# Emptying the bank of value products with one copy, two banks for it in one branch, and fillers moved ahead of a group's first product

## The chip, the core and the metric

The kernel runs on one core of a Trainium2 chip. A core has TensorE (matrix products, PE in the profile; its loading of stationary operands is listed apart as PEld), VectorE (DVE), ScalarE (ACT), GpSimd (POOL) and SyncE (SP), which issues the transfers. PE writes its results to PSUM, which has eight banks of 128 rows by 512 float32 values; everything else lies in SBUF, in tiles of 128 rows. The metric is the time of one execution on the device in microseconds.

## What is computed

One layer of a hybrid encoder on 1024 tokens of 1024 channels. A combined projection gives queries, keys and values for two groups of eight heads of 64 channels, and two gates. Branch A is a softmax over a band of 9 chunks of 64 with a learned bias; branch B is stick-breaking attention, causal and without a softmax. Both are projected, gated, merged and projected again; two layer norms and a SwiGLU block follow.

```
h = x @ w_in;  qa, ka, va, qb, kb, vb, ga, gb = split(h)
y_a = chunk_band_attention(qa, ka, va, rel_bias) @ w_proj_a
y_b = stick_breaking_attention(qb, kb, vb) @ w_proj_b
mix = (sigmoid(ga + b_a) * y_a + sigmoid(gb + b_b) * y_b) @ w_out
x = layer_norm(ALPHA * x + mix)
x = layer_norm(ALPHA * x + (silu(g) * u) @ w_ffn_out),  g, u = split(x @ w_ffn_in)

chunk_band_attention:     probs = softmax(q k / 8 + bias, within the band);  out = probs @ v
stick_breaking_attention: A[t, s] = beta_ts * prod_{s<j<t} (1 - beta_tj), beta = sigmoid(q k / 8);  out = A @ v
```

## The kernel before

Products are made in float32 split into a rounded part and a remainder (`split`, L102: a copy on ACT, then a subtraction on DVE, L103 and L104). The order of the tokens is reversed on the host, so that a causal sum runs forward.

The attention stage walks over 16 heads, eight of branch A and then eight of branch B. Two heads that follow each other, a pair, share one result tile `yt` of 128 rows (head `h` of the pair has rows `64 h` to `64 h + 63`) by 1024 queries. For each head the weights are made in eight blocks of 128 queries (`soft_block`, `stick_block`): scores on PE (L455, L456) into a bank of tag `sc`, then ACT and DVE, then POOL. In branch B the DVE part is a running product (L523, L527), whose second operand `ident_ps` lies in PSUM: it takes one bank of tag `tr` when the first block of branch B is made, which happens while the last head of branch A is still being finished, and keeps it.

The sums over the values are made in two groups of four query blocks, `g` 0 and 1, with eight and four steps, so twelve steps a head. A step (`value_steps`, L531) has two parts. `turn` transposes up to four blocks of weights on PE into a `tr` bank (L550) and splits them into a tile `pt` (tag of four tiles), which frees the bank. `mult`, which is called LAG = 2 steps later, multiplies `pt` with the values into the group's bank of tag `pv`. The stationary operand is 128 columns wide, 64 of the values' rounded part and 64 of their remainder, so the bank's rows 0 to 63 and 64 to 127 hold two parts of the same result, which have to be added. After a group's last step ACT copies rows 64 to 127 into `yt` (L569), and DVE adds rows 0 to 63 from PSUM to it (L570). Only then is the bank free for the next group's first product (L563).

PSUM is shared out as follows: two banks for `mm`, two for `sc`, three for `tr`, one for `pv`.

```
SLOTS = dict(bw=9, pt=4, yt=3, qs=2, kh=2, kl=2, v=2, gt=3, kp=4, op=8, xt=16)
BANKS = dict(mm=2, sc=2, tr=3, pv=1)
```

Between the parts of the steps stand fillers, matmuls of the remaining gates (L412) and of branch A's projection (L597), that need nothing of the present head. `fill_until` takes them from a generator, 18 per head of branch A and 42 per head of branch B (`FILL`), spread evenly over the twelve steps: half of a step's share behind its `turn`, half behind the `mult` that is called in that step. `LEAD` says how many blocks of weights are begun by each step, ahead of the step that uses them.

The written order is not quite the order on the engines. The framework plans the instructions with durations and buffers of its own, and where it expects a buffer to be in use it puts other instructions of the same engine first. Each engine then works through its queue in the planned order, with waits where an operand or a buffer is not ready.

Of the kernel before, what the change touches and what calls it, by code (L numbers as in the profile page):

```python
# [14 lines left out]
ALU = mybir.AluOpType  # L15
# [3 lines left out]
P = 128  # L19
# [3 lines left out]
DH = 64  # L23
# [8 lines left out]
LO, HI = slice(0, HW), slice(HW, 2 * HW)  # L32
# [14 lines left out]
def hybrid_trunk_kernel(ctx: ExitStack, tc, x, xt, w_in, b_gate, rel_bias, w_proj,  # L47
# [6 lines left out]
    nc = tc.nc  # L54
# [7 lines left out]
    def slot(tag, name, dtype=F32):  # L62
        return pool.tile([P, 1024], dtype, tag=tag, name=name, bufs=SLOTS[tag])
# [10 lines left out]
    def bank(tag, name):  # L74
        return ps.tile([P, HW], F32, tag=tag, name=name, bufs=BANKS[tag])
# [5 lines left out]
    tr = nc.tensor.transpose  # L81
# [20 lines left out]
    def split(dst_h, dst_l, src):  # L102
        nc.scalar.copy(dst_h, src)  # L103
        nc.vector.tensor_tensor(dst_l, src, dst_h.bitcast(F32), ALU.subtract)  # L104
# [324 lines left out]
    def load_qk(hd):  # L429

        i, h = hd["i"], hd["h"]
        n = 2 * i + h
        q, k = (d[i][h * P:(h + 1) * P] for d in (q_dr, k_dr))
        for key, part in (("qs", None), ("kh", 0), ("kl", DH)):
            t = hd[key] = slot(key, f"{key}{n}", F32R)
            if part is None:
                dma(t.bitcast(F32), q)
            else:
                for half in (slice(0, DH), slice(DH, P)):
                    dma(t[half].bitcast(F32), k[part:part + DH])  # L440
        if hd["br"] == 0:
            hd["bias"] = rel_bias_tile(hd["n"])

    def load_v(hd):

        n = 2 * hd["i"] + hd["h"]
        t = slot("v", f"v{n}", F32R)
        dma(t.bitcast(F32), v_dr[n])
        hd["v"] = t.rearrange("p (t c) -> p t c", t=8)
# [81 lines left out]
    def value_steps(hd, g, wt):  # L531

        br, h = hd["br"], hd["h"]
        reach = (4, 8)[br]
        q0 = 4 * g
        nm = f"{'ab'[br]}{hd['n']}_{g}"
        pv = []

        kbs = [4, 5, 6, 7, 3, 2, 1, 0] if g == 0 else [7, 6, 5, 4]
        steps = []  # L540
        for i, kb in enumerate(kbs):
            lo_q = max(q0, kb - reach)
            hi_q = min(q0 + 3, kb)
            n = (hi_q - lo_q + 1) * P
            pts = []

            def turn(kb=kb, lo_q=lo_q, hi_q=hi_q, n=n, pts=pts):
                tp = bank("tr", f"tp_{nm}_{kb}")
                for qb in range(lo_q, hi_q + 1):
                    tr(tp[:, (qb - lo_q) * P:(qb - lo_q + 1) * P],  # L550
                       wt[qb - q0][:, (kb - qb) * P:(kb - qb + 1) * P], ident)
                pt = slot("pt", f"pt_{nm}_{kb}", F32R)
                split(pt[:, 0:n], pt[:, HW:HW + n], tp[:, 0:n])
                pts.append(pt)

            def mult(i=i, kb=kb, lo_q=lo_q, n=n, pts=pts):
                v = hd["v"]
                if i == 0:
                    pv.append(bank("pv", f"pv_{nm}"))
                last = i == len(kbs) - 1  # L560
                cs = slice((lo_q - q0) * P, (lo_q - q0) * P + n)
                pt = pts[0]
                mm(pv[0][:, cs], v[:, kb, :], pt[:, 0:n], start=(i == 0), stop=False)  # L563
                mm(pv[0][:, cs], v[:, kb, :], pt[:, HW:HW + n], start=False, stop=last)
                if last:
                    yt = hd["yt"]()
                    r = slice(h * DH, (h + 1) * DH)
                    gs = slice(g * HW, (g + 1) * HW)
                    nc.scalar.copy(yt[r, gs], pv[0][DH:P])  # L569
                    nc.vector.tensor_tensor(yt[r, gs], pv[0][0:DH], yt[r, gs], ALU.add)  # L570
                    if h == 1 and g == 1 and hd["i"] < 7:
                        dma(y_dr[hd["i"]], yt)

            steps.append((turn, mult))
        return steps


# [56 lines left out]
    def fill_until(t):  # L634
        while state["t"] < t and not state["done"]:
            try:
                state["t"] += next(fill)
            except StopIteration:
                state["done"] = True
# [29 lines left out]
    pend = []  # L669
    steps_of = {}  # L670
    nhead = 12
    goal = 0.0
    load_qk(heads[0])
    load_v(heads[0])
    for si, (hd, g, st, box) in enumerate(vsteps):
        hidx, pos = si // nhead, si % nhead
        if hidx < 15 and pos == 1:
            load_qk(heads[hidx + 1])
        if hidx < 15 and pos == 4:
            load_v(heads[hidx + 1])  # L680
        while wi < min(hidx * 8 + LEAD[pos], len(wunits)):
            wunits[wi]()
            wi += 1
        if st == 0:
            steps_of[(hidx, g)] = value_steps(hd, g, box)
        turn, mult = steps_of[(hidx, g)][st]
        turn()
        last = goal
        goal += FILL[hd["br"]] / nhead
        fill_until(0.5 * (last + goal))  # L690
        pend.append(mult)
        if len(pend) > LAG:
            pend.pop(0)()
        fill_until(goal)
    for m_ in pend:
        m_()
    yh[7], yl[7] = slot("xt", "yh7", F32R), slot("xt", "yl7", F32R)
    split(yh[7], yl[7], last_yt[0])
# [226 lines left out]
```

## Time and profile before

| what | value |
|---|---|
| median of 3 runs | 1505.68 us (1505.52 to 1507.96) |
| the profiled execution | 1505.5 us, span 1503.5 us |
| projections, up to branch A's first value products | 0 to 359 us |
| branch A's value steps | 359 to 491 us |
| branch B's value steps | 493 to 684 us |
| everything after | 684 to 1503 us |
| groups drained | 16 in branch A, 16 in branch B |

In the profile a row of a wait reads "engine, tile, line <- engine, tile, line that released it: us in total, times, longest". A row in the order of time reads "start, duration, engine, line, operation, output <- inputs, shape, count", with the idle time of the engine before it and what ended it in brackets. Rows that follow each other on one engine and are of one kind are merged, so that the duration of two is given as one. PE rows overlap each other, since matmuls are pipelined; PEld rows are the loading of the stationary operand and run beside the matmul before.

### The profile page before, as it was taken

How to read it: one execution, taken by the hardware profiler on the slowest of the kernel's cores; microseconds unless marked ns; L12 is line 12 of the kernel's file. 1: busy time of each engine (PE TensorE's matmuls, PEld its weight loads, DVE VectorE, ACT ScalarE, POOL GpSimd, SP SyncE). 2: the span in 40 equal slices, each digit the busy share in tenths (PEclk: the TensorE clock that was granted, in tenths of full speed). 3: DMA queues.
4: the chain of work that ended last, by engine and by line, in shares of the span. 5: the costliest groups of instructions: out<-in, count | busy, mean ns of one | idle time of the engine just before them, and what ended most of it. 6: DMA issues, size and time to landing. Idle time of an engine off the chain costs nothing.

```text
span 1503.5 us, 18765 instructions
## 1 busy us (share of the span) xinstructions
PE 1455.7 (97%) x6824; PEld 1194.9 (79%) x6824; DVE 956.5 (64%) x1566; ACT 654.2 (44%) x1118; POOL 234.0 (16%) x290
## 2 busy tenths in 40 slices
PE   8999999999999999899999899999999999999997
PEld 6788888887887777777787688888888888888886
DVE  8865556436778887887749975555555447254437
ACT  6444444336778778775303643333333334021201
POOL 0000000004445568650014000000000000000016
PEclk9999999999999999999999999999999999999999
DMA  6555555247755556548402132222222248033202
GB/s 210 166 171 168 168 168 168 98 151 208 209 162 141 168 155 215 177 168 281 167 14 85 60 136 84 85 84 84 85 84 84 84 149 297 31 127 98 70 7 106
DMA packets 59324, 202.07 MB, mean 134 GB/s; under 512 B 7632, under 2 KB 7632, under 8 KB 59232
## 3 DMA queue, kind: packets, MB, share of 16 engines
q1 hardware_dynamic: 59232, 200.89, 41.2%
q8 instruction: 53, 0.87, 0.2%
q14 instruction: 39, 0.32, 0.1%
HBM read 141.06 MB, written 59.80 MB: 134 GB/s over the span
## 4 chain that ended last, share of the span: by engine, by line
PE 78%; DVE 11%; ACT 3%; DMA 3%; issue 3%; POOL 2%; SPq 0%; POOLq 0%; DVEq 0%; ACTq 0%
PE sxf L165 15%; PE sxp L165 11%; PE szf L165 8%; PE szp L165 6%; PE fps L113 5%; PE fps L110 5%; PE fps L111 5%; PE syf L165 4%; PE syp L165 3%; PE gps L412 2%; DVE kp_b L527 2%; PE ops L113 2%; PE ops L111 2%; PE ops L110 2%; PE yAps L597 1%
## 5 line engine op out<-in xcount | busy, mean ns | idle before, releaser
L739 POOL TENSOR_TENSOR mv<-mv,neghalf 128x1 f32<-128x1 f32 x16 | 23.4, 1460 | 760.6 <-DVE mv L738 760.6
L110 PE MATMUL fps<-wh_fo,wh_h 128*128 128x512 f32 x352 | 136.9, 389 | 0.0
L111 PE MATMUL fps<-wl_fo,wh_h 128*128 128x512 f32 x352 | 136.9, 389 | 0.0
L113 PE MATMUL fps<-wh_fo,wl_h 128*128 128x512 f32 x352 | 136.9, 389 | 0.0
L887 DVE TENSOR_TENSOR x<-fps,x 128x512 f32<-128x512 f32 x80 | 55.0, 689 | 96.2 <-PE fps L113 96.2
L529 POOL TENSOR_TENSOR w_b<-w_b,kp_b 128x511 f32<-128x511 f32 (+3 forms) x96 | 97.7, 1024 | 51.4 <-DVE kp_b L527 40.5
L527 DVE TENSOR_TENSOR_SCAN kp_b<-kp_b,ident_ps 128x384 f32<-128x384 f32 (+6 forms) x88 | 78.3, 890 | 4.1
L111 PEld LDWEIGHTS fps<-wl_fo,wh_h 128*128 128x128 f32 x352 | 66.1, 188 | 13.8
L113 PEld LDWEIGHTS fps<-wh_fo,wl_h 128*128 128x128 f32 x352 | 66.1, 188 | 13.6
L110 PEld LDWEIGHTS fps<-wh_fo,wh_h 128*128 128x128 f32 x352 | 66.1, 188 | 13.6
L395 ACT CAST wh_h<-wr_h 128x1024 fp32r<-128x1024 f32 x22 | 23.1, 1052 | 116.8 <-PE fps L111 50.7
L519 ACT ACTIVATE kp_b<-sc_b 128x512 f32<-128x512 f32 (+3 forms) x96 | 48.4, 504 | 31.4 <-PE sc_b L456 27.4
L178 DVE TENSOR_TENSOR c<-sxp,c 128x512 f32<-128x512 f32 x16 | 11.1, 691 | 74.8 <-issue 41.6
L104 DVE TENSOR_TENSOR pt_b<-tp_b,pt_b 128x512 fp32r<-128x512 f32 (+1 forms) x96 | 51.0, 542 | 11.0 <-ACT pt_b L103 10.5
L165 PE MATMUL szf<-x1S63h,wcf 128*128 128x512 f32 x176 | 57.8, 389 | 0.0
L550 PE MATMUL tp_b<-ident,w_b 128*128 128x128 f32 x288 | 49.4, 277 | 5.2 <-DVE pt_b L104 2.9
L473 POOL MEMSET bias<- 64x64 f32 x8 | 1.2, 145 | 334.1 <-ACT bias L472 334.1
L103 ACT CAST pt_b<-tp_b 128x512 fp32r<-128x512 f32 (+1 forms) x96 | 47.1, 497 | 13.9 <-PE tp_b L550 13.4
L494 POOL TENSOR_SCALAR w_a<-w_a,st_a 128x640 f32<-128x640 f32 (+2 forms) x64 | 42.6, 671 | 67.5 <-DVE st_a L493 49.9
L178 DVE TENSOR_TENSOR gt<-sxf,gt 128x512 f32<-128x512 f32 x22 | 15.1, 688 | 59.2 <-PE sxf L165 59.2
L113 PE MATMUL ops<-wh_o,ml 128*128 128x512 f32 x128 | 50.2, 392 | 0.2 <-DVE ml L104 0.2
L104 DVE TENSOR_TENSOR pt_a<-tp_a,pt_a 128x512 fp32r<-128x512 f32 (+1 forms) x96 | 45.4, 484 | 7.6 <-ACT pt_a L103 7.3
(1658 smaller groups left out, 4346.7 us busy)
## 6 DMA issues: line engine op xcount, KB each, us to landing
wLf<-in_w_ffn_in_dram SPq DMA_DIRECT2D x22, 512.0 KB, 3.5
wRf<-in_w_ffn_in_dram SPq DMA_DIRECT2D x22, 512.0 KB, 3.5
h_dr<-h SPq DMA_DIRECT2D x22, 512.0 KB, 2.6
wr_h<-h_dr SPq DMA_DIRECT2D x22, 512.0 KB, 4.4
wr_fo<-in_w_ffn_out_dram SPq DMA_DIRECT2D x22, 512.0 KB, 4.4
wLp<-in_w_in_dram SPq DMA_DIRECT2D x17, 512.0 KB, 5.2
wRp<-in_w_in_dram SPq DMA_DIRECT2D x17, 512.0 KB, 4.2
v_dr<-v SPq DMA_DIRECT2D x16, 512.0 KB, 4.2
```

What stands on the lines that cost most here:

```text
L103: nc.scalar.copy(dst_h, src)
L104: nc.vector.tensor_tensor(dst_l, src, dst_h.bitcast(F32), ALU.subtract)
L110: mm(acc, lh, rh, start=(i == 0), stop=False)
L111: mm(acc, lh, rl, start=False, stop=False)
L113: mm(acc, ll, rh, start=False, stop=(i == n))
L165: mm(acc, lw[:, ks], rx, start=(first and kt == i == 0), stop=(kt == 3 and i == 2), skip_group_check=not first)
L494: nc.gpsimd.tensor_scalar(s[:, 0:w], s[:, 0:w], st[:, 3:4], 0.0, ALU.mult, ALU.add)
L519: nc.scalar.activation(kp[:, c0:e], sc[:, 0:n], AF.Sigmoid, scale=-1.0)
L527: nc.vector.tensor_tensor_scan(kp[:, s0:e], kp[:, s0:e], ident_ps()[:, 0:e - s0], kp[:, s0 - 1:s0], ALU.mult, ALU.bypass)
L529: nc.gpsimd.tensor_tensor(be[:, m0:e], be[:, m0:e], kp[:, m0 - 1:e - 1], ALU.mult)
L550: tr(tp[:, (qb - lo_q) * P:(qb - lo_q + 1) * P], wt[qb - q0][:, (kb - qb) * P:(kb - qb + 1) * P], ident)
L887: nc.vector.tensor_tensor(acc_t[tt][:, cs], acc, acc_t[tt][:, cs], ALU.add)
```

## The change

Three things are changed in the attention stage.

First, the drain of a `pv` bank. ACT copies all 128 rows of the bank to SBUF, and DVE adds the two halves from there, so the bank has one reader. For the first head of a pair the copy goes to the pair's own `yt`, whose rows 64 to 127 are written later by the second head; for the second head it goes to a scratch tile `yv` from the same tag of three tiles, of which the first 512 columns are used. The addition's two inputs are then both in SBUF, rows 0 to 63 and rows 64 to 127.

Second, in branch A the second group of each head takes its bank from tag `tr`, so that the groups take it from `pv` and `tr` by turns. The number of banks of each tag stays. Branch B takes all from `pv`.

Third, before a group's first value product the rest of the step's fillers is taken ahead of the product; before, it stood behind it.

```diff
@@ value_steps
             def mult(i=i, kb=kb, lo_q=lo_q, n=n, pts=pts):
                 v = hd["v"]
                 if i == 0:
-                    pv.append(bank("pv", f"pv_{nm}"))
+
+                    pv.append(bank("tr" if br == 0 and g == 1 else "pv", f"pv_{nm}"))
                 last = i == len(kbs) - 1
...
                     gs = slice(g * HW, (g + 1) * HW)
-                    nc.scalar.copy(yt[r, gs], pv[0][DH:P])
-                    nc.vector.tensor_tensor(yt[r, gs], pv[0][0:DH], yt[r, gs], ALU.add)
+                    both, cs = (yt, gs) if h == 0 else (slot("yt", f"yv_{nm}"), LO)
+                    nc.scalar.copy(both[:, cs], pv[0])
+                    nc.vector.tensor_tensor(yt[r, gs], both[0:DH, cs], both[DH:P, cs], ALU.add)
                     if h == 1 and g == 1 and hd["i"] < 7:
                         dma(y_dr[hd["i"]], yt)
 
-            steps.append((turn, mult))
+            steps.append((turn, mult, i == 0))
         return steps
@@ the loop over the steps
-        turn, mult = steps_of[(hidx, g)][st]
+        turn, mult, begins = steps_of[(hidx, g)][st]
         turn()
         last = goal
         goal += FILL[hd["br"]] / nhead
         fill_until(0.5 * (last + goal))
-        pend.append(mult)
+        pend.append((mult, begins))
         if len(pend) > LAG:
-            pend.pop(0)()
+            m_, begins = pend.pop(0)
+            if begins:
+
+                fill_until(goal)
+            m_()
         fill_until(goal)
-    for m_ in pend:
+    for m_, _ in pend:
         m_()
```

## The prediction

> **What bounds the kernel now.** I read the page first, then busy time by stage, then who waited for whom in the two attention stages, then single drains in the order of time.
>
> ```profile
> PE 1455.7 (97%) x6824; PEld 1194.9 (79%) x6824; DVE 956.5 (64%) x1566; ACT 654.2 (44%) x1118; POOL 234.0 (16%) x290
> PE   8999999999999999899999899999999999999997
> ```
>
> TensorE (PE) is busy in nearly every slice, so the kernel can only get shorter where PE's remaining holes are. Busy time of each engine in the two stages that the change touches (branch A from 359 to 491 us, branch B from 505 to 684 us) says where these are:
>
> ```profile
> 359.00:491.00 132.00, 126.05 (x760) 106.21 (x759) 107.20 (x354) 104.93 (x262) 56.71 (x92) 1.00 0.61 171
> 505.00:684.00 179.00, 166.17 (x895) 133.81 (x896) 147.21 (x248) 136.24 (x292) 109.83 (x139) 1.00 0.56 177
> ```
>
> The columns are length, then PE, PEld, DVE, ACT, POOL. PE has 5.95 us without a matmul in A and 12.83 us in B; the granted clock is 1.00, so it plays no part. DVE is 82% busy in B, so it is the next engine in line. Who waited (total us, times, longest), branch A's rows first:
>
> ```profile
> PEld tp_a L550 <- DVE pt_a L104: 3.5, 7, 1.1
> PE tp_a L550 <- DVE pt_a L104: 2.3, 6, 0.9
> PE pv_a L563 <- DVE yt L570: 0.4, 1, 0.4
> ```
> ```profile
> PEld pv_b L563 <- DVE yt L570: 13.0, 13, 2.1
> PE pv_b L563 <- DVE yt L570: 8.1, 10, 1.6
> PEld tp_b L550 <- DVE pt_b L104: 7.8, 13, 1.1
> PE tp_b L550 <- DVE pt_b L104: 2.9, 6, 0.7
> ```
>
> In B the greatest wait of PE, 8.1 of its 12.83 us, is the first value product of a group (L563) waiting for the one `pv` bank, which the addition on DVE (L570) releases. One such drain, in order of time:
>
> ```profile
> 505.90 0.28 PE L564 MATMUL pv_b<-pt_b,v 128*128 128x128 f32 x1
> 506.62 0.58 ACT L569 COPY yt<-pv_b 64x512 f32<-64x512 f32 x1
> 507.33 0.39 PE L412 MATMUL gps<-xh,wh_g 128*128 128x512 f32 x1
> 507.56 0.40 PE L412 MATMUL gps<-xl,wh_g 128*128 128x512 f32 x1
> 507.69 0.53 DVE L104 TENSOR_TENSOR pt_b<-tp_b,pt_b 128x384 fp32r<-128x384 f32 x1
> 508.14 0.67 DVE L570 TENSOR_TENSOR yt<-pv_b,yt 64x512 f32<-64x512 f32 x1
> 508.74 0.40 DVE L523 TENSOR_TENSOR_SCAN kp_b<-kp_b,ident_ps 128x128 f32<-128x128 f32 x1
> 508.86 0.19 PEld L563 LDWEIGHTS pv_b<-pt_b,v 128*128 128x128 f32 x1 [1.33 <-DVE yt L570]
> 508.86 0.50 PE L563 MATMUL pv_b<-pt_b,v 128*128 128x512 f32 x1 [0.90 <-DVE yt L570]
> 509.17 0.61 DVE L527 TENSOR_TENSOR_SCAN kp_b<-kp_b,ident_ps 128x192 f32<-128x192 f32 x1
> 509.70 0.40 DVE L104 TENSOR_TENSOR pt_b<-tp_b,pt_b 128x256 fp32r<-128x256 f32 x1
> 511.05 0.59 PEld L550 LDWEIGHTS tp_b<-ident,w_b 128*128 128x128 f32 x4
> ```
>
> The last product of the old group ends at 506.18. ACT has its half out by 507.20. The addition stands behind other DVE work until 508.14 and ends at 508.81; the next group's product starts at 508.86. PE's loss lies between the two marks, 0.90 and 1.33. Over branch B it therefore lies between 8.1 and 13.0 us; I take the middle, 10.5.
>
> **The change part by part.** *The drain.* Each of the 32 groups keeps one ACT copy and one DVE addition; the copy takes 128 rows in place of 64, the addition reads SBUF alone in place of PSUM and SBUF. Groups by shape (busy us, mean ns), with the nearest rows of the new shapes:
>
> ```profile
> L569 ACT COPY yt<-pv_b 64x512 f32<-64x512 f32 x16 | 9.3, 582 | 0.6
> L191 ACT COPY c<-sxp 128x512 f32<-128x512 f32 x16 | 9.4, 589 | 29.3 <-PE sxp L165 29.3
> L570 DVE TENSOR_TENSOR yt<-pv_b,yt 64x512 f32<-64x512 f32 x16 | 10.8, 678 | 1.5 <-ACT yt L569 1.3
> L142 DVE TENSOR_TENSOR tbp<-wLp,tbp 128x512 f32<-128x512 f32 x16 | 10.9, 683 | 0.0
> ```
>
> So a copy grows by 7 ns and an addition by 5 ns: 0.2 us on each engine over 32 groups, beside PE work, taken as nothing. The bank is now free at the end of the copy, 507.20 in the drain shown. PE would have begun the product's weights at 507.53 (508.86 less the idle 1.33), so this wait goes entirely. It goes too in the longest stall of the stage:
>
> ```profile
> 633.07 0.58 ACT L569 COPY yt<-pv_b 64x512 f32<-64x512 f32 x1
> 636.02 0.19 PEld L563 LDWEIGHTS pv_b<-pt_b,v 128*128 128x128 f32 x1 [2.06 <-DVE yt L570]
> 636.99 0.40 DVE L104 TENSOR_TENSOR pt_b<-tp_b,pt_b 128x256 fp32r<-128x256 f32 x1
> 638.22 0.59 PEld L550 LDWEIGHTS tp_b<-ident,w_b 128*128 128x128 f32 x4
> ```
>
> There the copy ends at 633.65 and the product was wanted at 633.96. The margins are 0.33 and 0.31 us.
>
> What is late next: PE arrives earlier at the four transposes of the next head's first step, and these need a bank from which DVE's subtraction (L104) two steps back must have read. In the first drain that subtraction ends at 510.10 and the transposes start at 511.05, so PE can gain 0.95 us there at most; in the second it ends at 637.39 and they start at 638.22, 0.83 us. DVE's rows from 507.69 on follow one another without a hole, so it cannot bring that subtraction forward. The stalls themselves lie between 0.90 and 1.33 in the one, 1.63 (the longest of the PE row) and 2.06 in the other, with middles of 1.12 and 1.85. Of 2.97 us then 1.78 are kept, 60%. Of 10.5 us that is 6.3 us: my value for B. The bounds are 0 (DVE gives nothing back) and 13.0 (all of it).
>
> *The scratch tile.* For the odd head of a pair the copy goes to a tile of its own from the three `yt` slots. The pair's result holds one, two copies the others, and the earliest of them is long read when the next pair begins; no load waits for it, and the store of a pair (L572) is as far behind the addition as before. Nothing on SP's or POOL's queue moves.
>
> *The fillers.* Up to half a step's filler matmuls move from behind the first value product to ahead of it: 1.75 of them in B (42/12/2), 0.75 in A. Their number is the same, so PE's work is the same. In the drain shown two fillers follow each other at 507.33 and 507.56, 0.23 us apart, so 1.75 of them give the copy 0.40 us more, beside the margins of 0.33 and 0.31. I count no cost: what the product holds meanwhile, its `pt` tile, is one of four. Were the fourth `pt` tile missing, the step after would wait by those 0.40 us in each of 16 groups, 6.4 us over B.
>
> *Two tags in A.* A's own waits for the bank are 0.4 us by the PE row, and they go. That they are so few comes from the order on PE, which is not the written one:
>
> ```profile
> 404.26 0.20 PEld L550 LDWEIGHTS tp_a<-ident,w_a 128*128 128x128 f32 x2
> 405.67 0.58 ACT L569 COPY yt<-pv_a 64x512 f32<-64x512 f32 x1
> 406.37 0.67 DVE L570 TENSOR_TENSOR yt<-pv_a,yt 64x512 f32<-64x512 f32 x1
> 406.68 0.60 PE L550 MATMUL tp_a<-ident,w_a 128*128 128x128 f32 x4
> 406.97 0.41 DVE L104 TENSOR_TENSOR pt_a<-tp_a,pt_a 128x256 fp32r<-128x256 f32 x1
> 407.12 0.19 PEld L563 LDWEIGHTS pv_a<-pt_a,v 128*128 128x128 f32 x1
> ```
>
> The planner has put the next group's first product (407.12) behind transposes of two later steps (406.68), so the drain is covered by other work. The price of the second tag is a `tr` bank: while a second group of a head accumulates there, transposes have two banks in place of three, for some four of a head's twelve steps, 32 steps in all. Branch B shows what two banks cost, since `ident_ps` holds the third there: 2.9 us of PE waits over 96 steps, so 1.0 us over 32 steps; this I take, as the nearest row. Ends: at the worst the two transposes of 404.26 wait until the copy has emptied the bank at 406.25, 2.0 us in each of 7 heads, 14 us; at the best A's whole tp wait of 2.3 us goes with the new order.
>
> In the last head of A `ident_ps` has a `tr` bank already, and one is left for transposes:
>
> ```profile
> 485.90 0.33 PE L550 MATMUL tp_a<-ident,w_a 128*128 128x128 f32 x1 [0.40 <-DVE pt_a L104]
> 488.12 0.94 PE L550 MATMUL tp_b<-ident,w_b 128*128 128x128 f32 x4
> 488.99 0.27 DVE L104 TENSOR_TENSOR pt_a<-tp_a,pt_a 128x128 fp32r<-128x128 f32 x1
> ```
>
> The transposes at 488.12 would have to wait for the subtraction that ends at 489.26: 1.1 us, once. It may be nothing, if the planner finds other work, or three turns of it, 3.4.
>
> *The addition on DVE.* In the list from A the addition ends at 407.04 and the next DVE instruction starts at 406.97: they overlap by 0.07 us. I take no loss here. The Trainium skill, page "VectorE: DVE Perf Modes", section "Two Vector instructions with no wait between them", says that an instruction whose input or output starts in another 32-partition group than the last is held until all earlier ones have finished, and the new addition reads rows 0 to 63 and 64 to 127 of SBUF. No row of before has such a pair of inputs. By that rule each of B's 16 additions would lose that overlap, some 1.1 us on DVE, and were all of it on the path the sum would be 1.1 us higher.
>
> **The sum.** Against the profiled execution of 1505.5 us (span 1503.5; the median of the runs is 1505.68, 0.2 us off): minus 6.3 (B), minus 0.4 (A's wait), plus 1.0 (two banks in A), plus 1.1 (last head of A) is minus 4.6, so 1500.9 us.
>
> **The rivals.** *DVE takes the time back.* For it speaks DVE's 82% in B and the unbroken row of DVE work after each stall; against it the 0.95 and 0.83 us of room. B then gives 0, and the sum is 1505.5 - 0.4 + 2.1 = 1507.2.
>
> *A drain that is still late.* The margins are 0.3 us, and a copy that stands one ACT cast (0.58) later brings the wait back in part. If half of B's gain goes so, the time is 1505.5 - 3.2 - 0.4 + 2.1 = 1504.0; the change would then not do what it says, though the fillers' 0.4 us speak against it.
>
> *Branch A loses more by the third transpose bank than B gains* (slower). Place: the transposes just after a second group's last product. Price: up to 2.0 us a head. It ends above no change when 7 heads cost more than 6.3 + 0.4 - 1.1 = 5.6 us, 0.8 a head, and measurably above from 1.23. At 1.5 us a head the time is 1505.5 - 6.7 + 1.1 + 10.5 = 1510.4. Against it: PE had fillers, scores and other transposes to run in that very stretch. The Trainium skill, page "Perfetto Trace Analysis", section "Optimization Strategy", says that the same gap repeating can mean too little PSUM for the next tile; it fits the stalls in B as well as this rival, where the gap would appear at the transposes.
>
> **How the numbers follow.** Forecast 0.55, own range 1495 to 1503; DVE takes it back 0.15; late drain 0.12; slower by the bank 0.18. The range for all is 1495 (B near 10.5, A unchanged) to 1510 (the bank rival at about 1.5 a head). A measurement tells 0.2%, 3 us, from no change. Faster has nearly all of the forecast and a little of the late drain: 0.56. Same has the rest of these and most of the first rival: 0.24. Slower: 0.20.
>
> **What would show it.** Right: the row of L563 waiting for DVE L570 is gone, no row of it waiting for ACT above 2 us, and B's length falls by 5 to 7 us, with more waiting of transposes for DVE's `pt_b`. Wrong: A longer than 134 us with transposes waiting for ACT L569 or `pt_a`; a wait of L563 for ACT; or DVE rows in B with holes behind the addition. As the order on PE is planned anew, a loss outside both stages would also make the prediction wrong.

## The result and the profile after

The changed kernel takes 1510.65 us (median of 7 runs, 1508.55 to 1514.99), the kernel before 1505.19 us on the same chip (7 runs, 1503.9 to 1507.96). The ratio is 1.0038 with a 95% interval of 1.0024 to 1.0052: the change costs 0.4%. The prediction was 1500.9 us and faster. The profiled execution of the changed kernel has a span of 1508.1 us, against 1503.5. One execution each of `e2_tags`, `e6_psum_const` and `e9_scan_first` below was disturbed (1811.53, 2068.99 and 8307.96 us): the ratios leave it out, and the profile of `e6_psum_const`, which fell on it, is not shown.

In the totals of the page (busy time, share of the span, instructions), PE is nearly as it was, and DVE has grown by 11.5 us with the same number of instructions:

```profile
PE 1457.2 (97%) x6824; PEld 1196.8 (79%) x6824; DVE 968.0 (64%) x1566; ACT 649.8 (43%) x1118; POOL 237.3 (16%) x290
```

Busy time in the two stages (length, PE, PEld, DVE, ACT, POOL, clock):

```profile
359.00:491.00 132.00, 125.28 (x749) 104.58 (x747) 109.17 (x353) 101.34 (x258) 56.55 (x90) 1.00 0.60 170
505.00:684.00 179.00, 162.09 (x875) 132.08 (x874) 152.32 (x244) 130.40 (x286) 112.69 (x140) 0.99 0.54 170
```

In the same 179 us of branch B, PE does 162.09 us of work where it did 166.17, and DVE is busy for 152.32 where it was for 147.21. DVE has rather fewer instructions there (244 for 248) and needs 5 us more for them. The clock column of branch B has gone from 1.00 to 0.99. That is one stretch of 3.4 us at half the clock:

```profile
642.00:645.40 3.40, 3.29 (x11) 2.93 (x12) 2.58 (x5) 1.64 (x2) 1.99 (x3) 0.50 0.00 0
```

By estimate it costs at most 1.7 us (half of 3.4), and it begins at the end of the transposes' longest wait for DVE, 2.52 us. In the kernel before neither branch has such a stretch; what sets one off was not tried. Who waited in branch B (us in total, times, longest):

```profile
PE tp_b L550 <- DVE pt_b L104: 14.7, 13, 2.5
PEld tp_b L550 <- POOL w_b L529: 12.6, 8, 2.9
PEld tp_b L550 <- DVE pt_b L104: 8.2, 17, 1.1
PEld pv_b L564 <- ACT yv_b L571: 0.3, 1, 0.3
PEld pv_b L564 <- ACT yt L571: 0.2, 1, 0.2
```

The row that the change aimed at is gone: no value product waits for DVE any more, and for the new copy on ACT (L571) only 0.5 us. In its place the transposes wait for DVE's subtraction, 14.7 us where it was 2.9, and their loading for GpSimd's weights, 12.6 us where it was 2.2. GpSimd's own instruction is fed by DVE's scans (L527), but its total wait for them is no longer than before (29.3 us between 505 and 684 us, before 33.9), so the scans alone do not explain why GpSimd is late. The drain that the prediction showed reads, in order of time:

```profile
507.05 0.27 PE L565 MATMUL pv_b<-pt_b,v 128*128 128x128 f32 x1
507.61 0.65 ACT L571 COPY yt<-pv_b 128x512 f32<-128x512 f32 x1
508.83 0.53 DVE L104 TENSOR_TENSOR pt_b<-tp_b,pt_b 128x384 fp32r<-128x384 f32 x1
508.95 0.19 PEld L564 LDWEIGHTS pv_b<-pt_b,v 128*128 128x128 f32 x1
509.06 1.16 POOL L529 TENSOR_TENSOR w_b<-w_b,kp_b 128x448 f32<-128x448 f32 x1 [0.38 <-DVE kp_b L527]
509.40 1.37 DVE L572 TENSOR_TENSOR yt<-yt 64x512 f32<-64x512 f32 x1
510.69 0.41 DVE L523 TENSOR_TENSOR_SCAN kp_b<-kp_b,ident_ps 128x128 f32<-128x128 f32 x1
511.13 1.60 DVE L527 TENSOR_TENSOR_SCAN kp_b<-kp_b,ident_ps 128x192 f32<-128x192 f32 x2
512.65 0.40 DVE L104 TENSOR_TENSOR pt_b<-tp_b,pt_b 128x256 fp32r<-128x256 f32 x1
513.19 0.63 PE L550 MATMUL tp_b<-ident,w_b 128*128 128x128 f32 x4 [1.77 <-DVE pt_b L104]
```

The early part is as predicted. The bank is free at 508.26, the next product's weights load at 508.95 with no wait in front. But the addition takes 1.37 us where it took 0.67, and it began (509.40) while a multiplication on GpSimd (509.06 to 510.22) was under way. PE's gain of about a microsecond is given back at the transposes of 513.19, which stand idle for 1.77 us behind the subtraction of 512.65. A second thing differs: the subtraction (`pt_b`, 128x256) now stands behind the next block's second scan; in the kernel before it stood between the two scans (in the prediction's list of this drain the scan of 509.17 stands before it, and another follows at 510.02). So there were two suspects.

All additions of the changed kernel (duration in ns: least, median, greatest; then first and last start):

```profile
L572 DVE TENSOR_TENSOR yt<-yt x16: 686/774/2520, 367.6 to 674.1; 64x512 f32<-64x512 f32 x16
L572 DVE TENSOR_TENSOR yt<-yv_a x8: 689/690/1099, 382.5 to 493.2; 64x512 f32<-64x512 f32 x8
L572 DVE TENSOR_TENSOR yt<-yv_b x8: 689/1118/1384, 534.2 to 690.7; 64x512 f32<-64x512 f32 x8
```

The least is 686 ns, as predicted (683). Half of them are longer. Their busy time, by groups of line and shape, is 17.9 + 6.2 + 8.8 = 32.9 us; the kernel before had 10.9 + 10.8 = 21.7:

```profile
L572 DVE TENSOR_TENSOR yt<-yt 64x512 f32<-64x512 f32 x16 | 17.9, 1119 | 0.8 <-ACT yt L571 0.3
L572 DVE TENSOR_TENSOR yt<-yv_b 64x512 f32<-64x512 f32 x8 | 8.8, 1105 | 1.2 <-ACT yv_b L571 1.0
L572 DVE TENSOR_TENSOR yt<-yv_a 64x512 f32<-64x512 f32 x8 | 6.2, 778 | 0.5 <-ACT yv_a L571 0.2
```

Of 32 additions 16 take more than 0.75 us. Each of the 16 begins while a GpSimd instruction that reads SBUF is under way. Set against the time that this instruction still has to run, the durations lie on one line (us; the first two are the list above and the longest of all):

| addition at | GpSimd still runs for | addition takes | difference |
|---|---|---|---|
| 509.40 | 0.82 (L529) | 1.37 | 0.55 |
| 567.49 | 1.98 (L626) | 2.52 | 0.54 |
| 438.53 | 1.53 (L396) | 2.08 | 0.55 |
| 542.71 | 0.55 (L529) | 1.10 | 0.55 |
| 621.92 | 0.28 (L396) | 0.83 | 0.55 |
| 388.59 | 0.44 (L494) | 0.98 | 0.54 |

So the addition behaves as if it stood still until GpSimd is done and then took another 0.55 us. Two more additions began less than 0.12 us before the end of a GpSimd instruction and took 0.69 and 0.72. In the kernel before, where one input came from PSUM, 17 additions began inside such an instruction with more than 0.28 us to run (508.14 above: GpSimd runs from 507.91 to 509.04), and none was longer than 0.69 us. By the Trainium skill, page "SBUF — State Buffer", section "Who interferes with whom", a DVE instruction with two SBUF inputs contends with a GpSimd instruction that reads SBUF. The section "SBUF: two separate sides" of that page of the Trainium skill says that whichever of the two starts first gets the shared pair of ports for the whole instruction and that the other blocks. The table agrees with it on the blocking of DVE. The trace agrees on the other direction too, as one stretch shows:

```profile
516.08 2.40 POOL L396 TENSOR_TENSOR wl_y<-wr_y,wh_y 128x1024 fp32r<-128x1024 f32 x1 [0.22 <-PE gps L412]
517.79 1.24 DVE L572 TENSOR_TENSOR yt<-yt 64x512 f32<-64x512 f32 x1
518.43 1.48 POOL L529 TENSOR_TENSOR w_b<-w_b,kp_b 128x383 f32<-128x383 f32 x1
```

The addition stands behind the first GpSimd instruction, and the second one, which begins inside the addition, takes 1.48 us; in the kernel before the same multiplication took 1.01 us beside the old addition. Five multiplications of branch B begin inside an addition and take 0.43 to 0.46 us more than their shape usually takes, 2.2 us in sum. So GpSimd is late in part by the same lock.

### The profile page after: what moved, and what is told of

The parts are those of the page before. It is cut to its first block, busy times and chain, and to the rows that moved or that the text cites. A ratio compares the mean times of both kernels' runs of the same rounds, so it can differ in the third digit from the quotient of the medians.

```text
span 1508.1 us, 18751 instructions
## 1 busy us (share of the span) xinstructions
PE 1457.2 (97%) x6824; PEld 1196.8 (79%) x6824; DVE 968.0 (64%) x1566; ACT 649.8 (43%) x1118; POOL 237.3 (16%) x290
## 4 chain that ended last, share of the span: by engine, by line
PE 81%; DVE 11%; ACT 3%; issue 2%; POOL 1%; DMA 1%; POOLq 0%; SPq 0%; DVEq 0%; ACTq 0%
PE sxf L165 15%; PE sxp L165 11%; PE szf L165 8%; PE szp L165 6%; PE fps L110 5%; PE fps L111 5%; PE fps L113 5%; PE syf L165 4%; PE syp L165 3%; DVE kp_b L527 2%; PE gps L412 2%; PE yAps L599 2%; PE ops L113 2%; PE ops L111 2%; PE ops L110 2%
## 5 line engine op out<-in xcount | busy, mean ns | idle before, releaser
L529 POOL TENSOR_TENSOR w_b<-w_b,kp_b 128x511 f32<-128x511 f32 (+3 forms) x96 | 100.3, 1049 | 54.4 <-DVE kp_b L527 35.0
L527 DVE TENSOR_TENSOR_SCAN kp_b<-kp_b,ident_ps 128x384 f32<-128x384 f32 (+6 forms) x88 | 78.4, 891 | 4.6
L550 PE MATMUL tp_b<-ident,w_b 128*128 128x128 f32 x288 | 49.9, 280 | 17.6 <-DVE pt_b L104 14.7
L550 PEld LDWEIGHTS tp_b<-ident,w_b 128*128 128x128 f32 x288 | 34.1, 141 | 32.3 <-POOL w_b L529 12.6
L494 POOL TENSOR_SCALAR w_a<-w_a,st_a 128x640 f32<-128x640 f32 (+2 forms) x64 | 43.2, 679 | 67.8 <-DVE st_a L493 48.1
L110 PE MATMUL ops<-wh_o,mh 128*128 128x512 f32 x128 | 50.2, 392 | 0.0
```

The costliest lines, as they stand in the source:

```text
L110: mm(acc, lh, rh, start=(i == 0), stop=False)
L494: nc.gpsimd.tensor_scalar(s[:, 0:w], s[:, 0:w], st[:, 3:4], 0.0, ALU.mult, ALU.add)
L527: nc.vector.tensor_tensor_scan(kp[:, s0:e], kp[:, s0:e], ident_ps()[:, 0:e - s0], kp[:, s0 - 1:s0], ALU.mult, ALU.bypass)
L529: nc.gpsimd.tensor_tensor(be[:, m0:e], be[:, m0:e], kp[:, m0 - 1:e - 1], ALU.mult)
L550: tr(tp[:, (qb - lo_q) * P:(qb - lo_q + 1) * P], wt[qb - q0][:, (kb - qb) * P:(kb - qb + 1) * P], ident)
```

## The experiments

Three theories were to be told apart for the loss. *The lock*: the addition's second SBUF input makes it wait for GpSimd. *The banks* (K in some expectations): the `tr` bank that branch A gives away costs the time, the prediction's own rival. *The order* (O): the planner's new place for the subtraction costs it. A fourth, smaller one is that the two inputs start in different rows. Runs made together share a chip and a set of runs of the kernel before: 1504.5 us for the first four, 1504.33 for `e6`, `e8`, `e9` and `e11`, 1504.2 for the others. A line `...` in an edit marks what is left out.

**Part 1 alone: the drain.**

```diff
-                    nc.scalar.copy(yt[r, gs], pv[0][DH:P])
-                    nc.vector.tensor_tensor(yt[r, gs], pv[0][0:DH], yt[r, gs], ALU.add)
+                    both, cs = (yt, gs) if h == 0 else (slot("yt", f"yv_{nm}"), LO)
+                    nc.scalar.copy(both[:, cs], pv[0])
+                    nc.vector.tensor_tensor(yt[r, gs], both[0:DH, cs], both[DH:P, cs], ALU.add)
```

> The first part alone: one copy of 128 rows on ACT, then the addition from SBUF on DVE; tags and fillers as before. Theory L (the addition with both inputs in SBUF stands still while a GpSimd tensor_tensor on SBUF runs, so that DVE falls behind and the transposes wait for the subtraction two steps back): slower than before by 2 to 6 us, additions in branch B of about 1.4 us at the median, 10 us or more of PE waits of tp_b for DVE pt_b. Theory K (the loss is the bank that the second tag takes): faster by 3 us or more. Theory O (the loss is the order that the moved fillers bring): faster by 3 us or more.

Measured: 1512.25 us, ratio 1.0048 (1.0034 to 1.0062). The additions and the wait behind them:

```profile
L571 DVE TENSOR_TENSOR yt<-yt x16: 686/914/2523, 366.8 to 675.9; 64x512 f32<-64x512 f32 x16
L571 DVE TENSOR_TENSOR yt<-yv_b x8: 689/1118/1380, 535.9 to 692.5; 64x512 f32<-64x512 f32 x8
PE tp_b L550 <- DVE pt_b L104: 14.9, 13, 2.5
```

The whole loss comes with the drain alone, somewhat more than the 2 to 6 us that the theory of the lock expected, and with it the long additions. Branch B has two stretches at half the clock here (514.1 and 643.8, 3.4 us each), worth at most 3.4 us of the loss. The banks fall as its cause.

**Part 2 alone: two tags in branch A.**

```diff
-                    pv.append(bank("pv", f"pv_{nm}"))
+                    pv.append(bank("tr" if br == 0 and g == 1 else "pv", f"pv_{nm}"))
```

> The second part alone: the second group of a head in branch A takes its bank from tag tr. Theories L and O: within 2 us of before. Theory K: slower by 3 to 6 us, and the loss lies in branch A.

Measured: 1504.54 us, ratio 0.9998 (0.9989 to 1.0007): nothing. In branch A transposes wait 1.4 us for `pt_a` where they waited 2.3; in branch B the waits stay (8.1 us for the bank, 2.9 for `pt_b`).

**Part 3 alone: the fillers.** The old drain and tag, with the fillers taken ahead of a group's first value product.

```diff
...
+            if begins:
+                fill_until(goal)
+            m_()
```

> The third part alone: fillers ahead of a group's first value product, drain and tags as before. Theory L: faster by 2 to 6 us, since 1.75 fillers of 0.23 us go into 16 stalls of branch B (up to 6.4 us). Theory O: slower by 2 us or more. Theory K: as L.

Measured: 1503.41 us, ratio 0.9989 (0.998 to 0.9997), a gain of 1.1 us. The wait that it shortens was 8.1 us, 10 times:

```profile
PE pv_b L564 <- DVE yt L571: 6.9, 10, 1.4
```

So 1.2 us, or 0.08 for each of 16 groups. That is below what each theory had expected here (a gain or a loss of 2 us or more). The prediction had counted 0.40 us of margin a group; why so much less of it arrives was not tried.

**Parts 2 and 3, the old drain.**

> The second and the third part with the old drain. Theory L: faster by 2 to 6 us, the sum of the two alone; additions of 0.68 us throughout. Theories O and K: slower by 2 us or more, so that the drain isn't what makes the change slower.

Measured: 1503.91 us, ratio 0.9991 (0.9982 to 1.0). The changed kernel differs from this one by the drain alone and is 0.47% slower in relation to the kernel before, so the drain costs about 7 us on top of the other parts too. The gain of 0.09% is again below the 2 us expected.

**The drain with its second input from PSUM.** In branch B the addition takes its second input from `ident_ps`, a PSUM bank that is there anyway. All else is the changed kernel; the sum over the remainder rows is left out.

```diff
-                    nc.vector.tensor_tensor(yt[r, gs], both[0:DH, cs], both[DH:P, cs], ALU.add)
+                    nc.vector.tensor_tensor(yt[r, gs], both[0:DH, cs], aside[0][0:DH] if br else both[DH:P, cs], ALU.add)
```

> The changed kernel, but in branch B the addition takes ident_ps in PSUM as its second input in place of rows 64 to 127 of the copy (that half of the value product is left out). The bank is still free after the copy; the addition has one input in SBUF; and the planner puts the subtraction of step 10 ahead of the next block's last scan again, as before the change. Theories L (the addition stands still while GpSimd reads SBUF) and O (the subtraction of step 10 stands behind one scan more): faster than before by 2 to 8 us, additions of 0.68 us throughout. Theory Q (it is the early release itself that brings PE into other waits): still slower by 2 us or more.

Measured: 1501.2 us, ratio 0.9977 (0.9968 to 0.9986). With the lock gone the change is a gain of 0.2%. The planner also put the subtraction back to its old place here, so this run alone does not part lock from order.

**The same, with the order of the changed kernel.** As above, and the subtraction of step 10 is tied behind the second scan of the next head's fourth block.

```diff
...
+                scan = scans.get((hd["n"] + 1, 3)) if br == 1 and g == 1 and kb == 5 else None
+                with tc.issue_after(scan.ins) if scan else ExitStack():
+                    split(pt[:, 0:n], pt[:, HW:HW + n], tp[:, 0:n])
```

> As the kernel with ident_ps as second input (half of the value product of branch B left out), but the subtraction of step 10 is tied behind the last scan of the next head's block 3, so that DVE has the order of the changed kernel without its long additions. Theory L: within 2 us of before or faster. Theory O: slower than before by 3 us or more, near the changed kernel.

Measured: 1501.04 us, ratio 0.9978 (0.9969 to 0.9988). The additions, and the drain of before in order of time:

```profile
L575 DVE TENSOR_TENSOR yt<-yt,ident_ps x8: 665/670/680, 508.1 to 666.2; 64x512 f32<-64x512 f32 x8
L575 DVE TENSOR_TENSOR yt<-yv_b,ident_ps x8: 680/680/683, 532.2 to 682.0; 64x512 f32<-64x512 f32 x8
```
```profile
507.66 0.53 DVE L104 TENSOR_TENSOR pt_b<-tp_b,pt_b 128x384 fp32r<-128x384 f32 x1
507.89 1.15 POOL L530 TENSOR_TENSOR w_b<-w_b,kp_b 128x448 f32<-128x448 f32 x1 [0.39 <-ACT w_b L521]
508.11 0.67 DVE L575 TENSOR_TENSOR yt<-yt,ident_ps 64x512 f32<-64x512 f32 x1
508.70 0.40 DVE L524 TENSOR_TENSOR_SCAN kp_b<-kp_b,ident_ps 128x128 f32<-128x128 f32 x1
509.14 1.60 DVE L528 TENSOR_TENSOR_SCAN kp_b<-kp_b,ident_ps 128x192 f32<-128x192 f32 x2
510.66 0.40 DVE L104 TENSOR_TENSOR pt_b<-tp_b,pt_b 128x256 fp32r<-128x256 f32 x1
511.20 0.63 PE L551 MATMUL tp_b<-ident,w_b 128*128 128x128 f32 x4 [0.95 <-DVE pt_b L104]
```

DVE's order is that of the changed kernel (subtraction, addition, scan, two scans, subtraction). The addition begins 0.22 us into GpSimd's instruction, as there (0.34), and takes 0.67 us. The wait of the transposes at the end of the list falls from 1.77 to 0.95 us, by 0.82; the addition is 0.70 shorter. So the order alone costs nothing that the time shows (1501.04 us beside 1501.2 without it), and the lock with all that follows from it is worth 1.0038 - 0.9978 = 0.6%, 9 us. Branch B of `e9` has no stretch at half the clock, so up to 1.7 of the 9 us is the changed kernel's clock. The additions in branch B of the changed kernel exceed 0.69 us by 8.8 us in sum, and GpSimd loses its 2.2 us; how much of each reaches the end was not measured apart.

**The order of before, with the lock.** The changed kernel with the turn of step 10 written ahead of the next head's fourth block and that block's second scan tied behind the subtraction.

```diff
...
+                sub = subs.get((1, hd["n"] - 1, 1, 5)) if b == 3 and c0 else None
+                with tc.issue_after(sub.ins) if sub else ExitStack():
+                    nc.vector.tensor_tensor_scan(kp[:, s0:e], kp[:, s0:e], ident_ps()[:, 0:e - s0],
+                                                 kp[:, s0 - 1:s0], ALU.mult, ALU.bypass)
...
```

> The changed kernel with its addition from two SBUF inputs, but in branch B step 10 is turned ahead of the next head's block 3 and that block's last scan is tied behind the subtraction of step 10, so the subtraction stands ahead of the scans. Theory L: additions still up to 1.37 us and slower than before by 2 us or more. Theory O: faster than before by 2 to 8 us.

Measured: 1510.27 us, ratio 1.0036 (1.0023 to 1.0049), the loss of the changed kernel. The additions are long as there (16 of 32 above 0.75 us). Most of the wait for the subtraction went, and others took its place:

```profile
L575 DVE TENSOR_TENSOR yt<-yv_b x8: 690/1122/1464, 533.5 to 691.9; 64x512 f32<-64x512 f32 x8
PE tp_b L553 <- POOL w_b L513: 6.8, 5, 1.4
PE tp_b L553 <- POOL w_b L532: 4.3, 3, 1.8
PE tp_b L553 <- DVE pt_b L104: 2.8, 5, 0.7
```

The three waits sum to 13.9 us. Whichever DVE does first, the scans (which feed GpSimd) or the subtraction, PE waits for the other; the order chooses the name in the waits. The new order falls as the cause: without it the loss stays (`e11`), and with it but without the lock there is none (`e9`). That it is worth nothing beside the lock is not shown, since branch B has three stretches at half the clock here, two more than the changed kernel (at most 3.4 us).

**Both inputs in SBUF, from the same rows.** The addition reads rows 0 to 63 twice and leaves out rows 64 to 127. Every queue has the order of the changed kernel.

```diff
-                    nc.vector.tensor_tensor(yt[r, gs], both[0:DH, cs], both[DH:P, cs], ALU.add)
+                    nc.vector.tensor_tensor(yt[r, gs], both[0:DH, cs], both[0:DH, cs], ALU.add)
```

> The changed kernel, but the addition takes rows 0 to 63 of the copy twice (rows 64 to 127 are left out): two SBUF inputs that start at the same row. All queues have the order of the changed kernel. Theories L and O: as slow as the changed kernel, 4 to 7 us above before, additions up to 1.37 us again. If the different rows of the two inputs make the addition long: faster than the changed kernel by 3 us or more, additions of 0.69 us.

Measured: 1509.11 us, ratio 1.0032 (1.0021 to 1.0043), which can't be told from the changed kernel's 1.0038.

```profile
L572 DVE TENSOR_TENSOR yt<-yv_b x8: 684/1115/1380, 533.6 to 690.0; 64x512 f32<-64x512 f32 x8
```

That the rows differ is not what makes the additions long.

**No GpSimd multiplication in branch B.** The changed kernel without the instruction that multiplies the weights with the running product (L529), so branch B's weights lack that factor.

```diff
-            nc.gpsimd.tensor_tensor(be[:, m0:e], be[:, m0:e], kp[:, m0 - 1:e - 1], ALU.mult)
```

> The changed kernel without GpSimd's multiplication in branch B (L529, the weights stay without their running product). The theory of the lock: additions of branch B of 0.69 us, but for those few that meet a GpSimd subtraction of a weight or of y. If something else makes the additions long: as many of 1.1 to 1.4 us as in the changed kernel.

Measured: 1498.86 us in one run.

```profile
L571 DVE TENSOR_TENSOR yt<-yv_b x8: 687/689/691, 532.1 to 680.1; 64x512 f32<-64x512 f32 x8
```

Both inputs are in SBUF, in different rows, and with GpSimd mostly idle 15 of branch B's 16 additions take 0.69 to 0.70 us; the other one began inside a GpSimd instruction of the weights' splitting (L396) and took 1.31. The time itself says less, since work was taken away.

**The old drain, given time instead.** If the bank can't be freed early without the lock, the product can be asked for later: the old drain with tags and fillers, and a group's first value product one step later.

```diff
...
-        if len(pend) > LAG:
+        while len(pend) > LAG + pend[0][1]:
```

> A version meant to beat both: the old drain (the addition reads PSUM and SBUF), tags and fillers of the change, and a group's first value product one step later, so that it follows the drain by a whole step. The theory that the addition's lock is what costs, and that the old wait for the bank is worth some 4 us in branch B: no wait of L564 for DVE above 2 us in all, and faster than before by 3 to 8 us. If the wait only moves to the transposes: within 2 us of before.

Measured: 1500.45 us, ratio 0.9977 (0.9967 to 0.9987), faster than both kernels and with the whole computation.

```profile
L571 DVE TENSOR_TENSOR yt<-pv_b,yt x16: 654/683/684, 507.1 to 681.6; 64x512 f32<-64x512 f32 x16
PEld pv_b L564 <- DVE yt L571: 0.5, 1, 0.5
PE tp_b L550 <- DVE pt_b L104: 5.0, 13, 0.7
```

The waits of the value products are gone, the additions are short, and the transposes wait 5.0 us for `pt_b`.

**The same with one tag.**

```diff
-                    pv.append(bank("tr" if br == 0 and g == 1 else "pv", f"pv_{nm}"))
+                    pv.append(bank("pv", f"pv_{nm}"))
```

> As the version with the first value product one step later, but all groups take their bank from tag pv. If the second tag is worth little, as alone: within 1.5 us of that version.

Measured: 1501.39 us, ratio 0.9977 (0.9968 to 0.9986). The second tag isn't needed for the gain.

## Why the prediction was wrong

**The step that failed is the drain:** "So a copy grows by 7 ns and an addition by 5 ns: 0.2 us on each engine over 32 groups, beside PE work, taken as nothing". The addition grew by some 10 ns where GpSimd was idle (678 to 689), and in the sum over 32 by 11.2 us (32.9 less 21.7), 8.8 us of the excess over 0.69 in branch B. The duration came from row L142, whose form fits but whose stage, the projections before 308 us, leaves GpSimd idle (0.73 us busy); in branch B it is busy for 109.83 of 179 us. What the additions met there is the lock of the table above. The warning stood in the profile of before. The splitting instruction on DVE with two SBUF inputs takes 1.21 to 1.23 us in all 22 cases between 1231 and 1420 us, where GpSimd does nothing, and 1.20 us at 672.13 in branch B, but 1.67 us where it begins inside a GpSimd instruction:

```profile
663.98 0.88 POOL L529 TENSOR_TENSOR w_b<-w_b,kp_b 128x320 f32<-128x320 f32 x1 [0.23 <-DVE kp_b L527]
664.27 1.67 DVE L396 TENSOR_TENSOR wl_y<-wr_y,wh_y 128x1024 fp32r<-128x1024 f32 x1
```

And a GpSimd multiplication that began inside the other one (672.36) took 1.57 us, where its shape usually takes 0.74.

And "beside PE work" failed with it: the prediction itself saw DVE's instructions follow one another without a hole and let PE keep only 60% of its gain for that reason, but the price of an instruction in that row without holes was looked up as if it stood alone.

The lengths of the stages show where it went. Branch A is taken from the first value product to the end of the last, branch B from there to the end of its last. Before, after, and `e9` (the lock out of branch B):

```profile
489.92 0.30 PE L564 MATMUL pv_a<-pt_a,v 128*128 128x128 f32 x1
684.01 0.28 PE L564 MATMUL pv_b<-pt_b,v 128*128 128x128 f32 x1
```
```profile
491.61 0.31 PE L565 MATMUL pv_a<-pt_a,v 128*128 128x128 f32 x1
688.92 0.28 PE L565 MATMUL pv_b<-pt_b,v 128*128 128x128 f32 x1
```
```profile
490.44 0.31 PE L568 MATMUL pv_a<-pt_a,v 128*128 128x128 f32 x1
680.19 0.28 PE L568 MATMUL pv_b<-pt_b,v 128*128 128x128 f32 x1
```

| kernel | A begins | A, us | B, us |
|---|---|---|---|
| before | 359.60 | 130.6 | 194.1 |
| after | 359.04 | 132.9 | 197.3 |
| `e1_drain` | 358.29 | 132.9 | 199.8 |
| `e2_tags` | 359.49 | 131.8 | 193.3 |
| `e4_tags_fill` | 357.81 | 131.8 | 192.5 |
| `e9_scan_first` | 357.85 | 132.9 | 189.7 |
| `e10_later` | 359.26 | 130.4 | 190.8 |

These are single executions; where A begins differs by up to 1.8 us between kernels that do the same until then, so differences of a microsecond are not read from it.

- *Branch B's gain, forecast 6.3 us.* The mechanism is right: the bank's wait goes in full, and the transposes' wait for `pt_b` is what is late next. Without the lock B is 4.4 us shorter. The term was too large by about 2 us; in `e9`'s drain the transposes wait 0.95 us. With the lock B is 3.2 us longer, of which the stretch at half the clock is at most 1.7; the prediction had said of the clock that it plays no part.
- *Branch A, forecast +1.7 us in three terms.* A is 2.3 us longer. The tags alone give +1.2 in A, and `e2_tags` as a whole shows no loss. The drain alone gives +2.2, with the bank's tag unchanged. The two do not add, so the shares of the 2.3 us stay open. A's additions exceed 0.69 us by 2.1 us in sum (0.98, 2.08 and 1.10 us are the long ones), so the lock is a candidate in A too; `e9` left it in there, and no run took it out with the new drain kept.
- *The fillers, forecast nothing.* They are worth 1.1 us without the new drain.
- *The scratch tile, forecast nothing.* No wait for it is in the profile; no run tried the drain without it.
- *The start rows of the inputs.* The prediction took no loss and priced the Trainium skill's rule at 1.1 us. The trace does show the hold: the addition of the changed kernel begins 0.04 us after the subtraction before it ends (508.83 + 0.53, then 509.40); in `e9` it begins 0.08 before that end. But in the kernel before, the additions of each pair's second head, whose SBUF input and output start in row 64, already begin 0.03 us after that end. So the hold is new for only 8 of branch B's 16 additions: with 0.12 us each it is 1.0 us at most. Where GpSimd blocks the addition anyway it is hidden: `e8`, where the first heads' additions are not held, has the same time.
- *The rivals.* "DVE takes the time back" named the right engine, but for the wrong reason and with a floor of zero: it had branch B gain nothing, where B is 3.2 us longer. The bank rival gave the time best, 1510.4, by luck: its mechanism is refuted by `e2_tags`. A time that fits is no proof of its reason.

The change as it is loses some 5.5 us; freed of the lock in branch B it would win 3.3 (`e9`, which leaves out part of the sum). A version with the whole sum, the early release and no lock was not found: with this addition on DVE beside a busy GpSimd, one of the two inputs would have to be in PSUM, which is what holds the bank.

## What to carry to other kernels

Before a DVE instruction's input moves from PSUM to SBUF, look at what GpSimd does in that stage, and take its duration from a row of the same stage: beside a busy GpSimd an instruction with two SBUF inputs can cost twice what it costs alone, and more (0.69 us alone, 1.37 in the drain shown, 2.52 at the worst). Here the buffer was freed early by giving an engine that works without holes a dearer instruction, and that moved the wait and made it longer. Where a buffer is asked for too early, asking for it a step later may bring as much: `e10_later` (0.9977, with the whole sum) and `e9` (0.9978, the early release with the lock out of branch B) end alike. `e10_later` also has the moved fillers, which alone gained 1.1 us; the step without them was not tried.

## What the runs showed of the hardware

A DVE addition of 64x512 with both inputs in SBUF that begins inside a GpSimd instruction reading SBUF ends 0.55 us after that instruction does; alone it takes 0.69 us. It is so for three kinds of GpSimd work: multiplications of two tensors (L529), subtractions (L396, L626) and a tensor by a scalar (L494). With one input in PSUM none of it is seen (0.65 to 0.69 us in all of the old additions). A GpSimd multiplication that begins inside such an addition is held in its turn: with 128x383 it takes 1.45 to 1.48 us in four cases, 1.02 elsewhere, and 1.01 to 1.05 inside the old additions with one input in PSUM.

TensorE's granted clock falls to 0.50 for 3.4 us once in branch B of the changed kernel (642.0), where matmuls of 512 columns start 0.43 us apart in place of 0.23; it falls twice there in `e1_drain`, three times in `e11_sub_first`, and not at all in the kernel before, `e9` and `e10_later`.
